# The feed-forward block's seven-product scheme: weight sums by adding transfers, and its first product behind the third plain chunk

## The chip, the core and the metric

One core of one Trainium2 chip runs the whole kernel. The metric is the device time in microseconds (us). Before the change it is 491.46 us, the median of 3 runs (491.43 to 491.74). Engines are called PE (TensorE: matrix multiplication), DVE (VectorE), ACT (ScalarE), POOL (GpSimd) and SP (SyncE, which issues most transfers here). Each engine works through its own list of instructions in order and waits on semaphores for the others.

## The reference

The kernel computes one decoder block for 256 tokens of width 1024: a gated linear recurrence and a block attention read the same normalised input, their outputs are gated, summed and projected, and a SwiGLU feed-forward block follows. Only that last block matters here (D = 1024, D_FF = 2816):

```
h2 = rmsnorm(x, ffn_norm_g[l])
x = x + (jax.nn.silu(h2 @ w_ffn_gate[l]) * (h2 @ w_ffn_up[l])) @ w_ffn_down[l]
```

## The kernel before

**Precision.** All products are float32 in effect. A float32 tensor is split into a high half (`whi`, made by an ACT copy to the reduced form float32r) and a low half (`wlo`, a DVE subtraction of the high half from the original); three products of halves replace one. `split` (L54 to L56) does this for activations and weights alike. A megabyte of weights (128 x 2048 elements) therefore costs one ACT copy and one DVE subtraction before PE can use it. The pools of halves (`whi`, `wlo`) and of raw weights (`wraw`) have three buffers each, so at most three blocks of weights are split ahead of PE or in use by it; a raw block is loaded by SP as soon as a raw buffer is free, that is, when an earlier block has been split.

**The feed-forward block.** Of the 2816 hidden columns the first 1792 (`NPL` = 14 tiles of 128) go the plain way, the last 1024 through a seven-product scheme.

- *Plain chunks.* `plain` (L798) makes gate and up columns in blocks of 512: two chunks of half the depth for the gate, two for the up weights. Each chunk is one call of `step(next, chunks_a)`, one load of 1 MB, one split, and 32 matmuls (16 of 512 columns at L102, 16 of 256 at L101 and L105). There are twelve such chunks, called c1 to c12 here, three blocks of four. After the second chunk of each pair the four PSUM banks are folded (L121, L122). A last short block (`rest`) follows.
- *The scheme.* `scheme` (L831) multiplies the 256 tokens by a 1024 x 1024 block of weights, cut into quarters W11, W12, W21, W22 of 512 x 512 and the tokens into halves. Instead of eight products of quarters it takes seven, P1 to P7, of sums of token blocks with sums of weight quarters. `quarter` (L629) loads a quarter (1 MB, SP), `halves` (L635) splits it, `product` (L641) issues 12 matmuls of 512 columns (L645). The token sums are made once by `token_sums2` (L783: four DVE operations of 128 x 512 and two splits) and serve both schemes. The weight sums are made by DVE, in place, between the products: four subtractions of 128 x 2048 (L841, L848, L853, L859) in each scheme.
- *Order.* The gate scheme is interleaved by hand with the twelve chunks: a string gives the order, "c" for a chunk and "P" for a product. Before, it is "ccPcPccPccPccPcPcPc". The up scheme is interleaved with the down projection's steps (`down`, one load of w_down, 24 matmuls at L903 to L905), one step before each product; PE goes D0, P1, D1, P2, D2, P3, D3, P4, D4 and so on.
- `tc.issue_after(x)` puts the instructions of its block behind x on x's engine. `step` uses it to keep PE to the written order. The lists of the other engines, the queues' included, are laid out by the framework from the written order and from when it expects operands to be free, so they may differ from the written order.

The tiles `T8` to `T11` hold the four quarters, first for the gate weights, then for the up weights; a quarter's load waits until the last reader of its tile is done.

Of the kernel before, what the change touches and what calls it, by code (L numbers as in the profile page):

```python
# [7 lines left out]
F32 = mybir.dt.float32  # L8
F32R = mybir.dt.float32r
U32 = mybir.dt.uint32  # L10
AF = mybir.ActivationFunctionType
OP = mybir.AluOpType
AX = mybir.AxisListType

P = 128
S = 256
# [11 lines left out]
def tile_hgrn2_moba_block(ctx: ExitStack, tc: tile.TileContext, xm, xw, table, runs,  # L28
                          w_in, w_hg, w_at, w_out, w_gate, w_up, w_down, out):
    nc = tc.nc  # L30
# [3 lines left out]
    small = ctx.enter_context(tc.tile_pool(name="small", bufs=1))  # L34
# [3 lines left out]
    def pw(name="pw"):  # L38
        return psum.tile([P, 512], F32, name=name, tag="pw", bufs=4)

    def ph(name="ph"):
        return psum.tile([P, 512], F32, name=name, tag="ph", bufs=2)

    def pa(name="pa"):
        return psum.tile([P, 512], F32, name=name, tag="pa", bufs=2)
# [8 lines left out]
    def split(src, hi, lo):  # L54
        high = nc.scalar.copy(hi, src)  # L55
        return high, nc.vector.tensor_sub(lo, src, hi.bitcast(F32))  # L56

    halved = []
# [80 lines left out]
    for kt in range(KT):  # L139
        n0 = 0 if kt == 0 else NV  # L140
        t = big.tile([P, NX + D - n0], F32, name=f"xw{kt}", tag=("T3", "T4", "T5", "T1", "T7", "T8", "T9", "T11")[kt])
# [29 lines left out]
    for kt in range(KT):  # L171
        i = kt % 2
# [11 lines left out]
        else:  # L184
# [3 lines left out]
                                       op0=OP.mult, op1=OP.subtract)  # L188
# [18 lines left out]
    for j in range(7):  # L207
        c = 1 << j
# [212 lines left out]
    def hgrn_out(A01):  # L421
        o = big.tile([P, 2, D], F32, name="o", tag="T2")
        so = small.tile([P, 2, H], F32, name="so")
        for tb in range(2):
            for g in range(2):
# [10 lines left out]
                nc.scalar.activation(o2.rearrange("p h t -> p (h t)"), bank, AF.Square)  # L436
                nc.vector.tensor_reduce(so[:, tb, 4 * g:4 * g + 4], o2, axis=AX.X, op=OP.add)
        ro = small.tile([P, 2, H], F32, name="ro")
# [81 lines left out]
    def softmax(nm, sc, w):  # L520
        mx = small.tile([P, H], F32, name="mx" + nm)
        nc.vector.tensor_reduce(mx, sc, axis=AX.X, op=OP.max)
        nc.vector.tensor_scalar_mul(mx, mx, -1.0)
# [74 lines left out]
    def branch_gate(br, half):  # L598
        ps = tok_block(w_in, 7168 + br * D + half * 512, XT)
        for tb in range(2):  # L600
            nc.scalar.activation(G[br][:, tb, half * 512:(half + 1) * 512], ps[tb], AF.Sigmoid,
                                 scale=rx[:, tb:tb + 1])
# [26 lines left out]
    def quarter(i, j, tag, w=w_in, c0=g0):  # L629
        t = big.tile([P, 4, 512], F32, name=f"W{i}{j}", tag=tag)  # L630
        nc.sync.dma_start(t, w[i * 512:(i + 1) * 512, c0 + j * 512:c0 + (j + 1) * 512]
                          .rearrange("(k p) c -> p k c", p=P))
        return t

    def halves(raw):  # L635
        hi = wp.tile([P, 4, 512], F32R, name="whi")
        lo = wp.tile([P, 4, 512], F32R, name="wlo")
        halved.append(split(raw, hi, lo))
        return hi, lo

    def product(bank, act, w, first):  # L641
        hi, lo = w
        for kt in range(4):
            for m, h in ((0, hi), (0, lo), (1, hi)):
                mm = nc.tensor.matmul(bank, act(kt, m), h[:, kt, :], start=(first and kt == 0 and m == 0 and h is hi),  # L645
                                      stop=(kt == 3 and m == 1), skip_group_check=True)
        tail[0] = mm
        return mm

    def tokens(i, j, act=XT):  # L650
        return lambda kt, m: act[j][:, kt, m, i * P:(i + 1) * P]

    def summed(c, of=None):
        return lambda kt, m: (of or sums)[m][c][:, kt, :]
# [5 lines left out]
    sums = token_sums()  # L660
    W11 = quarter(0, 0, "T9")
    W12 = quarter(0, 1, "T1")
    branch_gate(1, 1)
    turn_a, b1, turn_h, b3 = pa("turn"), pa("b1"), ph("turn"), ph("b3")
    product(b1, tokens(0, 0), halves(W11), True)
    oT, put_oT, at = hgrn_gate(o, ro, sg, (turn_a, turn_h, pw("turn"), pw("turn")))

    def then(f, *args):
        with tc.issue_after(at.ins):
            return f(*args)  # L670
# [24 lines left out]
    def gq(i, j):  # L695
        return G[0][:, i, j * 512:(j + 1) * 512]
# [4 lines left out]
    nc.scalar.copy(gq(1, 0), b1)  # L701
    nc.vector.tensor_sub(W11, W12, W11)
    step0, out0 = at_block(0)
    at = then(step0)
    at = then(product, b3, summed(0), halves(W11), True)
    W22 = quarter(1, 1, "T8")
    at = then(step0)
    with tc.issue_after(halved[-1][1].ins):
        nc.vector.tensor_sub(W11, W22, W11)
        low = nc.vector.tensor_sub(W12, W22, W12)  # L710
    put_oT(halved[-1][0], low)
    b2 = pa("b2")
    at = then(product, b2, summed(1), halves(W11), True)
    W21 = quarter(1, 0, "T2")
# [4 lines left out]
    with tc.issue_after(halved[-1][1].ins):  # L719
        out0()  # L720
        nc.vector.tensor_add(gq(0, 1), b2, gq(1, 0))
    at = then(product, b2, summed(2), halves(W12), False)
    nc.vector.tensor_add(gq(1, 1), b2, gq(1, 0))
# [32 lines left out]
    x2f = big.tile([P, 2, 4, S], F32, name="x2f", tag="T2")  # L756
    ss2 = small.tile([P, 2, 2], F32, name="ss2")
    for half in range(2):
        ps = tok_block(w_out, half * 512, M)
        for tb in range(2):  # L760
# [8 lines left out]
            x2_split = split(xg, x2T[half][:, :, 0, tb * P:(tb + 1) * P], x2T[half][:, :, 1, tb * P:(tb + 1) * P])  # L769
            jk2 = big.tile([P, 512], F32, name="jk2", tag="T15")  # L770
            nc.scalar.activation(jk2, xs, AF.Square, accum_out=ss2[:, tb, half:half + 1])
    r2 = small.tile([P, 2], F32, name="r2")
# [8 lines left out]
    SC = NPL * P  # L781

    def token_sums2():  # L783
        C = big.tile([P, 4, 4, P], F32, name="C2", tag="T3")
        hi = big.tile([P, 4, 4, P], F32R, name="C2h", tag="T4")
        lo = big.tile([P, 4, 4, P], F32R, name="C2l", tag="T5")
        nc.vector.tensor_add(C[:, 0], x2f[:, 0, :, P:S], x2f[:, 1, :, P:S])
        nc.vector.tensor_sub(C[:, 1], C[:, 0], x2f[:, 0, :, 0:P])
        nc.vector.tensor_sub(C[:, 2], x2f[:, 0, :, 0:P], x2f[:, 0, :, P:S])
        nc.vector.tensor_sub(C[:, 3], x2f[:, 1, :, 0:P], C[:, 1])  # L790
        for i in range(2):
            split(C[:, 2 * i:2 * i + 2], hi[:, 2 * i:2 * i + 2], lo[:, 2 * i:2 * i + 2])
        return [hi[:, c] for c in range(4)], [lo[:, c] for c in range(4)]

    def step(f, *args):
        with tc.issue_after(tail[0].ins):
            return f(*args)
# [32 lines left out]

    def scheme(w, banks, p1, at_out, q):  # L831

        X = x2T
        W11 = quarter(0, 0, "T10", w, SC)
        W21 = quarter(1, 0, "T9", w, SC)
        W12 = quarter(0, 1, "T11", w, SC)
        W22 = quarter(1, 1, "T8", w, SC)
        b1 = banks()
        product(b1, tokens(0, 0, X), halves(W11), True)
        nc.scalar.copy(p1, b1)  # L840
        nc.vector.tensor_sub(W11, W12, W11)  # L841
        yield
        product(b1, tokens(0, 1, X), halves(W21), False)
        at_out(0, 0, b1)
        yield
        b3 = banks()
        product(b3, summed(0, sums2), halves(W11), True)
        nc.vector.tensor_sub(W11, W22, W11)  # L848
        yield
        b2 = banks()  # L850
        product(b2, summed(1, sums2), halves(W11), True)
        nc.vector.tensor_add(q(0, 1), b2, p1)
        nc.vector.tensor_sub(W12, W22, W12)  # L853
        yield
        product(b2, summed(2, sums2), halves(W12), False)
        nc.vector.tensor_add(q(1, 1), b2, p1)
        nc.vector.tensor_add(q(1, 1), q(1, 1), b3)
        at_out(1, 1, q(1, 1))
        nc.vector.tensor_sub(W21, W21, W11)  # L859
        yield  # L860
        product(b3, summed(3, sums2), halves(W22), False)
        nc.vector.tensor_add(q(0, 1), q(0, 1), b3)
        at_out(0, 1, q(0, 1))
        yield
        product(b2, tokens(1, 1, X), halves(W21), False)
        nc.vector.tensor_add(q(1, 0), b2, p1)
        at_out(1, 0, q(1, 0))
        yield
# [53 lines left out]
    def gq2(i, j):  # L922
        return sG[:, i, j * 512:(j + 1) * 512]

    def silu(i, j, src):
        nc.scalar.activation(gq2(i, j), src, AF.Silu, scale=r2[:, i:i + 1])

    ring = iter([pa, ph, pa])
    blocks = iter([c for b in range(3) for c in [plain(4 * b, 4, b)]])
    chunks_a = (c for g in blocks for c in g)  # L930
    with tc.issue_after(x2_split[0].ins), tc.issue_after(x2_split[1].ins):
        sums2 = token_sums2()
    gate = scheme(w_gate, lambda: next(ring)("g"), gq2(1, 0), silu, gq2)
    for what in "ccPcPccPccPccPcPcPc":
        if what == "c":
            step(next, chunks_a)
        else:
            with tc.issue_after(x2_split[0].ins), tc.issue_after(x2_split[1].ins):
                step(next, gate)
    assert not list(chunks_a) and not list(gate)  # L940
    rest = plain(12, 2, 3)
    for _ in range(4):
# [5 lines left out]
    def uq(i, j):  # L948
        return U[:, i, j * 512:(j + 1) * 512]

    def hidden(i, j, src):
        nc.vector.tensor_mul(uq(i, j), src, gq2(i, j))

    def turn(i, j):
        bank = pw("turn")
# [85 lines left out]
```

## Time and profile before

| | before |
|---|---|
| median of 3 runs | 491.46 us |
| profiled execution: its own time | 492.7 us |
| profiled execution: span | 491.0 us |
| PE busy | 484.0 us (99%) |
| DVE busy | 397.8 us (81%) |
| ACT busy | 301.5 us (61%) |
| POOL busy | 24.8 us (5%) |
| moved by transfers | 91.16 MB, mean 186 GB/s |
| granted TensorE clock | 0.999 |

The profile is of one execution. A row of the timeline gives start and duration in us, the engine, the source line, the operation, out<-in by tile names, shapes, the count, and in brackets how long the engine had been idle before it and what it waited for. PE's matmuls overlap in the pipeline: a 512-column matmul is shown with 0.39 us, while the next one starts 0.23 us later. A row of the table of waits gives the total, the number of times and the longest wait. A transfer's issue row ends with the median time from issue to landing. The feed-forward block begins at about 306 us of the span.

### The profile page before, as it was taken

The numbers are of one execution on the slowest core, as the hardware profiler recorded it, in microseconds if no ns is written. First come the engines' busy times: TensorE is split into PE (matmuls) and PEld (weight loads), VectorE is DVE, ScalarE is ACT, GpSimd is POOL, SyncE is SP. The second block draws the span as 40 slices with busy tenths as digits, with TensorE's granted clock in tenths as the row PEclk, the third lists the DMA queues.
The fourth block names the chain that finished last, engine by engine and source line by source line (L and its number), as shares of the span: only waits on it lengthen the run. The fifth ranks groups of instructions, "written<-read, shape, count | busy, mean of one in ns | idle before, by whom it ended". The sixth has DMA issues, their size and how long they took to land.

```text
span 491.0 us, 6512 instructions
## 1 busy us (share of the span) xinstructions
PE 484.0 (99%) x2598; PEld 407.4 (83%) x2598; DVE 397.8 (81%) x426; ACT 301.5 (61%) x402; POOL 24.8 (5%) x59
## 2 busy tenths in 40 slices
PE   8999999999999999999999999989999999999997
PEld 6888888888888888988888878878888888888885
DVE  5768999697779979499987777999978779986843
ACT  5977746777748984875564445866565566454520
POOL 0930220000000000000000000000000000000000
PEclk9999999999999999999999999999999999999999
DMA  8977595724524448418367577433785564352402
GB/s 303 402 238 258 166 313 178 240 90 143 201 87 145 137 137 274 167 46 297 90 237 274 175 258 259 165 117 141 241 261 179 176 257 156 102 172 85 171 1 85
DMA packets 42142, 91.16 MB, mean 186 GB/s; under 512 B 1656, under 2 KB 3960, under 8 KB 42112
## 3 DMA queue, kind: packets, MB, share of 16 engines
q1 hardware_dynamic: 41376, 88.11, 52.7%
q0 software_dynamic: 736, 2.65, 1.7%
q8 instruction: 20, 0.33, 0.3%
q14 instruction: 10, 0.08, 0.0%
HBM read 89.67 MB, written 1.07 MB: 185 GB/s over the span
## 4 chain that ended last, share of the span: by engine, by line
PE 94%; DVE 4%; DMA 1%; ACT 0%; SPq 0%; issue 0%
PE pw L102 15%; PE pw L84 10%; PE pw L86 10%; PE pw L85 10%; PE pw L168 4%; PE acc L905 4%; PE acc L904 4%; PE acc L903 4%; PE pw L645 4%; PE b L645 4%; PE pw L105 4%; PE pw L101 4%; PE g L645 3%; PE pw L684 1%; PE pw L685 1%; PE pw L683 1%
## 5 line engine op out<-in xcount | busy, mean ns | idle before, releaser
L56 DVE TENSOR_TENSOR wlo<-wraw,whi 128x2048 fp32r<-128x2048 f32 (+1 forms) x69 | 149.0, 2164 | 39.2 <-ACT whi L55 39.0
L55 ACT CAST whi<-wraw 128x2048 fp32r<-128x2048 f32 (+1 forms) x69 | 124.7, 1813 | 61.7 <-PE pw L86 32.3
L102 PE MATMUL pw<-x2T,whi 128*128 128x512 f32 x224 | 71.8, 396 | 0.0
L56 DVE TENSOR_TENSOR wlo<-W,whi 128x2048 fp32r<-128x2048 f32 x21 | 47.9, 2287 | 11.1 <-ACT whi L55 11.0
L84 PE MATMUL pw<-whi,XT 128*128 128x512 f32 x144 | 56.9, 395 | 0.0
L55 ACT CAST whi<-W 128x2048 fp32r<-128x2048 f32 x21 | 40.2, 1913 | 26.5 <-PE acc L905 13.6
L86 PE MATMUL pw<-whi,XT 128*128 128x512 f32 x144 | 56.2, 390 | 0.0
L85 PE MATMUL pw<-wlo,XT 128*128 128x512 f32 x144 | 56.1, 390 | 0.0
L102 PE MATMUL pw<-XT,whi 128*128 128x512 f32 x128 | 40.6, 395 | 0.0
L102 PEld LDWEIGHTS pw<-x2T,whi 128*128 128x128 f32 x224 | 35.1, 189 | 0.5
L105 PE MATMUL pw<-x2T,wlo 128*128 128x256 f32 x112 | 31.3, 279 | 1.6 <-DVE wlo L56 1.6
L86 PEld LDWEIGHTS pw<-whi,XT 128*128 128x128 f32 x144 | 27.0, 188 | 5.7
L84 PEld LDWEIGHTS pw<-whi,XT 128*128 128x128 f32 x144 | 27.0, 188 | 5.6
L85 PEld LDWEIGHTS pw<-wlo,XT 128*128 128x128 f32 x144 | 27.1, 188 | 5.4
L101 PE MATMUL pw<-x2T,wlo 128*128 128x256 f32 x112 | 31.2, 279 | 0.0
L105 PEld LDWEIGHTS pw<-x2T,wlo 128*128 128x128 f32 x112 | 21.1, 188 | 6.5 <-DVE wlo L56 2.0
L101 PEld LDWEIGHTS pw<-x2T,wlo 128*128 128x128 f32 x112 | 21.0, 188 | 5.0
L903 PE MATMUL acc<-whi,hT 128*128 128x512 f32 x56 | 21.9, 391 | 0.0
L905 PE MATMUL acc<-whi,hT 128*128 128x512 f32 x56 | 21.8, 390 | 0.0
L904 PE MATMUL acc<-wlo,hT 128*128 128x512 f32 x56 | 21.8, 389 | 0.0
L102 PEld LDWEIGHTS pw<-XT,whi 128*128 128x128 f32 x128 | 19.8, 189 | 0.2
L168 PE MATMUL pw<-whi,XT 128*128 128x512 f32 x64 | 18.1, 400 | 0.7 <-ACT whi L186 0.7
(357 smaller groups left out, 1020.8 us busy)
## 6 DMA issues: line engine op xcount, KB each, us to landing
wraw<-w_in SPq DMA_DIRECT2D x26, 1024.0 KB, 5.1
wraw<-w_down SPq DMA_DIRECT2D x11, 1024.0 KB, 4.9
wraw<-w_gate SPq DMA_DIRECT2D x6, 1024.0 KB, 5.0
wraw<-w_up SPq DMA_DIRECT2D x6, 1024.0 KB, 5.1
wraw<-w_at SPq DMA_DIRECT2D x4, 1024.0 KB, 6.4
W<-w_in SPq DMA_DIRECT2D x4, 1024.0 KB, 5.3
wraw<-w_hg SPq DMA_DIRECT2D x4, 1024.0 KB, 5.7
W<-w_gate SPq DMA_DIRECT2D x4, 1024.0 KB, 6.0
```

The lines of the kernel that those rows point to most:

```text
L55: high = nc.scalar.copy(hi, src)
L56: return high, nc.vector.tensor_sub(lo, src, hi.bitcast(F32))
L84: nc.tensor.matmul(ps[tb], part(act, kt, 0)[:, ts], wh, start=(kt == 0), stop=False)
L85: nc.tensor.matmul(ps[tb], part(act, kt, 0)[:, ts], wl, start=False, stop=False)
L86: nc.tensor.matmul(ps[tb], part(act, kt, 1)[:, ts], wh, start=False, stop=(kt == KT - 1))
L101: nc.tensor.matmul(ps[ct][:, 0:S], lo[:, i, cs], part(act, kt, 0), start=False, stop=False)
L102: wide = nc.tensor.matmul(ps[ct], hi[:, i, cs], both, start=(kt == 0), stop=(kt == KT - 1))
L105: tail[0] = nc.tensor.matmul(ps[ct][:, 0:S], lo[:, i, cs], part(act, kt, 0), start=False, stop=False)
L645: mm = nc.tensor.matmul(bank, act(kt, m), h[:, kt, :], start=(first and kt == 0 and m == 0 and h is hi), stop=(kt == 3 and m == 1), skip_g ...
L903: nc.tensor.matmul(acc[tb][half], act[:, j, 0, ts], hi[:, i, cs], start=st, stop=False)
L904: nc.tensor.matmul(acc[tb][half], act[:, j, 0, ts], lo[:, i, cs], start=False, stop=False)
L905: tail[0] = nc.tensor.matmul(acc[tb][half], act[:, j, 1, ts], hi[:, i, cs], start=False, stop=en)
```

## The change

- The token sums change signs: the first is x2[1] − x2[0] of the second token half where it was a sum, and the second and fourth are formed by a scalar-tensor form (negate, then subtract). With that, every weight sum of the scheme is a plain sum. The second column half of the result comes out negated; `silu` takes a negated scale for it (`r2n`, one new operation of 128 x 2) and `hidden` multiplies by −1 in a scalar-tensor form.
- The eight DVE weight sums are gone. In their place a transfer on GpSimd's queue reads a quarter from HBM and adds it to a tile that holds another (`add`). Y is W11 loaded a second time; it becomes Y + W12 for P3, then + W22 for P4, then + W21 for P7. T3 is W22 loaded a second time, + W12, for P5. So each scheme has five plain loads on SP (W11, W21, Y, W22, T3) where it had four, and four adding transfers. Each is 1 MB.
- The order string becomes "cccsPcPccPcPccPcPcPc", where "s" makes the token sums. P1 moves from behind c2 to behind c3, P2 from behind c3 to behind c4, P3 from behind c5 to behind c6; P4 stays behind c7. The token sums and products are issued behind the split of c3, and c3 behind the split of the last token block.

```diff
@@ token_sums2
-        nc.vector.tensor_add(C[:, 0], x2f[:, 0, :, P:S], x2f[:, 1, :, P:S])
-        nc.vector.tensor_sub(C[:, 1], C[:, 0], x2f[:, 0, :, 0:P])
+        nc.vector.tensor_sub(C[:, 0], x2f[:, 1, :, P:S], x2f[:, 0, :, P:S])
+        nc.vector.scalar_tensor_tensor(C[:, 1], C[:, 0], -1.0, x2f[:, 0, :, 0:P], op0=OP.mult, op1=OP.subtract)
         nc.vector.tensor_sub(C[:, 2], x2f[:, 0, :, 0:P], x2f[:, 0, :, P:S])
-        nc.vector.tensor_sub(C[:, 3], x2f[:, 1, :, 0:P], C[:, 1])
+        nc.vector.scalar_tensor_tensor(C[:, 3], C[:, 1], -1.0, x2f[:, 1, :, 0:P], op0=OP.mult, op1=OP.subtract)
@@ scheme
+        def add(t, i, j):
+            nc.gpsimd.dma_start(t, w[i * 512:(i + 1) * 512, SC + j * 512:SC + (j + 1) * 512]
+                                .rearrange("(k p) c -> p k c", p=P), accum_op=OP.add)
+
         W11 = quarter(0, 0, "T10", w, SC)
         W21 = quarter(1, 0, "T9", w, SC)
-        W12 = quarter(0, 1, "T11", w, SC)
+        Y = quarter(0, 0, "T11", w, SC)
+        add(Y, 0, 1)
         W22 = quarter(1, 1, "T8", w, SC)
         b1 = banks()
         product(b1, tokens(0, 0, X), halves(W11), True)
         nc.scalar.copy(p1, b1)
-        nc.vector.tensor_sub(W11, W12, W11)
         yield
         product(b1, tokens(0, 1, X), halves(W21), False)
         at_out(0, 0, b1)
+        T3 = quarter(1, 1, "T10", w, SC)
+        add(T3, 0, 1)
         yield
         b3 = banks()
-        product(b3, summed(0, sums2), halves(W11), True)
-        nc.vector.tensor_sub(W11, W22, W11)
+        product(b3, summed(0, sums2), halves(Y), True)
+        add(Y, 1, 1)
         yield
         b2 = banks()
-        product(b2, summed(1, sums2), halves(W11), True)
+        product(b2, summed(1, sums2), halves(Y), True)
         nc.vector.tensor_add(q(0, 1), b2, p1)
-        nc.vector.tensor_sub(W12, W22, W12)
+        add(Y, 1, 0)
         yield
-        product(b2, summed(2, sums2), halves(W12), False)
+        product(b2, summed(2, sums2), halves(T3), False)
...
-        nc.vector.tensor_sub(W21, W21, W11)
...
-        product(b2, tokens(1, 1, X), halves(W21), False)
+        product(b2, tokens(1, 1, X), halves(Y), False)
@@ silu, hidden and the order
-        nc.scalar.activation(gq2(i, j), src, AF.Silu, scale=r2[:, i:i + 1])
+        nc.scalar.activation(gq2(i, j), src, AF.Silu, scale=(r2, r2n)[j][:, i:i + 1])
+    r2n = small.tile([P, 2], F32, name="r2n")
+    nc.vector.tensor_scalar_mul(r2n, r2, -1.0)
-    with tc.issue_after(x2_split[0].ins), tc.issue_after(x2_split[1].ins):
-        sums2 = token_sums2()
-    for what in "ccPcPccPccPccPcPcPc":
+    third, chunk_no = None, 0
+    for what in "cccsPcPccPcPccPcPcPc":
         if what == "c":
-            step(next, chunks_a)
-        else:
             with tc.issue_after(x2_split[0].ins), tc.issue_after(x2_split[1].ins):
+                step(next, chunks_a) if chunk_no == 2 else None
+            if chunk_no != 2:
+                step(next, chunks_a)
+            third = third or (halved[-1] if chunk_no == 2 else None)
+            chunk_no += 1
+            continue
+        with tc.issue_after(third[0].ins), tc.issue_after(third[1].ins):
+            if what == "P":
                 step(next, gate)
+            else:
+                sums2 = token_sums2()
-        nc.vector.tensor_mul(uq(i, j), src, gq2(i, j))
+        nc.vector.scalar_tensor_tensor(uq(i, j), src, (1.0, -1.0)[j], gq2(i, j), op0=OP.mult, op1=OP.mult)
```

## The prediction

> **What bounds the kernel now.** I read the page first, for busy shares and the chain that ended last.
>
> ```profile
> span 491.0 us, 6512 instructions
> ...
> PE 484.0 (99%) x2598; PEld 407.4 (83%) x2598; DVE 397.8 (81%) x426; ACT 301.5 (61%) x402; POOL 24.8 (5%) x59
> ...
> PE 94%; DVE 4%; DMA 1%; ACT 0%; SPq 0%; issue 0%
> ```
>
> TensorE (PE) is busy 484.0 of 491.0 us and the change leaves its multiplications as they are, so only its idle time can be won, 7.0 us in all. The windows view (stretch, length, then each engine's busy time, PE first) places it.
>
> ```profile
> 0.00:20.00 20.00, 18.20 (x76) 14.95 (x77) 12.71 (x32) 13.28 (x26) 8.58 (x22) 1.00 0.91 345
> 320.00:330.00 10.00, 8.40 (x45) 6.91 (x44) 10.00 (x9) 6.77 (x7) 0.00 (x0) 1.00 0.35 109
> 480.00:491.00 11.00, 7.36 (x39) 6.14 (x37) 3.94 (x6) 0.00 (x0) 0.00 (x0) 0.97 0.26 95
> ```
>
> PE idles 1.8 us at the start, 3.6 at the end and 1.6 in one hole between 320 and 330 us, with DVE busy all 10.0; these are the 7.0. Only the hole lies in the feed-forward stage, which alone the change touches. The table of waits and PE's timeline show it.
>
> ```profile
> PE pw L105 <- DVE wlo L56: 1.6, 1, 1.6
> ```
> ```profile
> 318.36 0.39 PE L645 MATMUL g<-whi,x2T 128*128 128x512 f32 x1
> ...
> 321.08 1.08 PE L102 MATMUL pw<-x2T,whi 128*128 128x512 f32 x4
> 323.76 0.39 PE L105 MATMUL pw<-x2T,wlo 128*128 128x256 f32 x1 [1.60 <-DVE wlo L56]
> ...
> 328.56 0.39 PE L645 MATMUL g<-whi,x2T 128*128 128x512 f32 x1
> ...
> 331.29 0.39 PE L102 MATMUL pw<-x2T,whi 128*128 128x512 f32 x1
> ...
> 342.44 0.39 PE L645 MATMUL g<-whi,C2h 128*128 128x512 f32 x1
> ```
>
> From 318.36 PE runs P1, from 321.08 the third plain chunk c3, from 328.56 P2, then c4 and c5 from 331.29 to 342.44. Two undisturbed chunks took 11.15 us, so one takes 5.57 and a product (318.36 to 321.08) 2.72. Chunk c3 took 328.56 − 321.08 = 7.48: **1.9 us too long**, because the low half of its weights came late. VectorE's (DVE) timeline says why.
>
> ```profile
> 309.49 0.68 DVE L787 TENSOR_TENSOR C<-x2f 128x512 f32<-128x512 f32 x1
> ...
> 311.30 2.28 DVE L56 TENSOR_TENSOR wlo<-W,whi 128x2048 fp32r<-128x2048 f32 x1
> ...
> 315.82 2.28 DVE L841 TENSOR_TENSOR W<-W,W 128x2048 f32<-128x2048 f32 x1
> ...
> 318.36 1.21 DVE L56 TENSOR_TENSOR C2l<-C,C2h 128x1024 fp32r<-128x1024 f32 x1
> ...
> 321.42 2.28 DVE L56 TENSOR_TENSOR wlo<-wraw,whi 128x2048 fp32r<-128x2048 f32 x1
> ```
> ```profile
> 308.75 1.91 ACT L55 CAST whi<-W 128x2048 fp32r<-128x2048 f32 x1
> ...
> 313.02 1.90 ACT L55 CAST whi<-wraw 128x2048 fp32r<-128x2048 f32 x1
> ```
>
> ScalarE had c3's high half at 314.9, after P1's (308.75), but DVE reached the low half (321.42) only after the token sums (309.49 to 318.36), P1's split and the first weight sum. DVE, not PE, was the bound for this stretch alone.
>
> **Part 1: c3 ahead of P1, token sums behind c3.** The split of c3 now takes the place, and the third weight buffer, that P1's split had: high half at 308.75, low half at 311.30 or sooner, so it is there by 313.6, and PE reaches c3 when c2 ends, at 318.36: 4.8 us of room where there was a hole. What is late next? P1's split: it needs c1's buffer, free when c2 begins, at the latest 318.36 − 5.57 = 312.8, and P1 now starts at 318.36 + 5.57 = 323.93; eleven us for 1.9 + 2.28. The token sums (four additions like the 0.68 and two splits like the 1.21, 5.1 us) are first used by P3 at 346. Adjacent c2 and c3 both need four PSUM banks, but c4 and c5 are such a pair and show no hole. Gain: **−1.9 us**. Between nothing (DVE's folds of c2 fill the place) and −1.9 I take −1.9, since 9.7 us of DVE work (5.1, P1's 2.28, the weight sum's 2.28) leave the stretch ahead of c3's low half and the room is 4.8.
>
> **Part 2: eight weight sums leave DVE.**
>
> ```profile
> L859 DVE TENSOR_TENSOR W<-W,W 128x2048 f32<-128x2048 f32 x2 | 4.6, 2286 | 0.0
> ...
> L841 DVE TENSOR_TENSOR W<-W,W 128x2048 f32<-128x2048 f32 x2 | 4.6, 2282 | 0.0
> ```
>
> These are the last and the first of four such groups: 8 × 2.28 = 18.3 us of DVE. Worth nothing beyond part 1, since PE has no other hole before the end of the span. The two scalar-tensor forms in the token sums, the negated r2 and the sign in `hidden` replace operations of equal size one for one, or add one on 128 x 2; I set them at nothing, covered by the 18.3 us given up.
>
> **Part 3: the adds.** Each scheme issues five plain loads on SP (four before) and four adds on GpSimd, 1 MB each. Nothing in the trace adds in a transfer. Nearest rows:
>
> ```profile
> wraw<-w_down SPq DMA_DIRECT2D x11, 1024.0 KB, 4.9
> ...
> x<-xm POOLq DMA_DIRECT2D x1, 1024.0 KB, 5.2
> ...
> line_d<-line POOLq DMA_DIRECT2D x1, 24.0 KB, 2.1
> ```
>
> A plain megabyte on GpSimd's queue lands after 5.2 us, 24 KB after 2.1, so the megabyte itself is 3.1. An add must read the tile as well as the source: two passes make 2.1 + 6.2 = 8.3 us, and three passes (two reads and a separate write) 11.4. The lower bound is 5.2. [...]
>
> Most adds have long cover. In the second scheme (up) Y's first load takes the buffer that a load had late in the list of before:
>
> ```profile
> 383.23 0.37 SPq L631 DMA_DIRECT2D W<-w_up  x1
> ```
>
> From there 5.2 and an add of up to 12.8 end near 401, and P3's split is at 420. Y's last add has P5 and P6 ahead of P7, T3's has P3 and P4 ahead of P5. The tight one is **Y += W22, between P3's split and P4's split**. It can't start before P3's halves are made (they read Y), and P4's halves can't start before it lands. In the up scheme:
>
> ```profile
> 420.00 1.92 ACT L55 CAST whi<-W 128x2048 fp32r<-128x2048 f32 x1 [3.04 <-PE acc L905]
> ...
> 428.21 1.92 ACT L55 CAST whi<-W 128x2048 fp32r<-128x2048 f32 x1 [3.57 <-PE acc L905]
> 430.93 1.92 ACT L55 CAST whi<-wraw 128x2048 fp32r<-128x2048 f32 x1 [0.80 <-PE pw L645]
> ```
> ```profile
> 421.95 2.29 DVE L56 TENSOR_TENSOR wlo<-W,whi 128x2048 fp32r<-128x2048 f32 x1 [1.17 <-ACT whi L55]
> ...
> 426.96 2.28 DVE L56 TENSOR_TENSOR wlo<-wraw,whi 128x2048 fp32r<-128x2048 f32 x1
> ```
> ```profile
> 436.12 0.39 PE L645 MATMUL pw<-whi,C2h 128*128 128x512 f32 x1
> 436.35 0.39 PE L645 MATMUL pw<-wlo,C2h 128*128 128x512 f32 x1
> ```
>
> P3's split ends at 421.95 + 2.29 = 424.24 and waits for PE's buffer (420.00), not for DVE, so it can't come earlier. P4's second matmul, at 436.35, needs a low half, 1.92 + 2.29 after the add landed: by 432.14. The window is **7.9 us**. (All of this moves by the 1.9 together.) The add takes 8.3 alone, and w_down's load for a later step is issued when DVE ends the low half at 426.96, which without the sum ahead of it moves up by 2.28 to about 427, into the middle of the add. Sharing the engines with that load's 4.9 − 2.1 = 2.8 us costs the add about half of it, 1.4. So 9.7 us, 1.8 more than the window: **+1.8 us** on PE at P4. Ends: 5.2 gives 0; 11.4 + 1.4 = 12.8 gives 4.9. Behind P4's waiting split on ScalarE stands the next step's (430.93); PE asks for it only when P4 has ended, 2.72 us after P4's start, however late that is, so its own 1.92 and 2.28 stay covered.
>
> In the first scheme (gate) there is a chunk pair ahead of P3, so its split is earlier:
>
> ```profile
> 334.01 2.29 DVE L56 TENSOR_TENSOR wlo<-W,whi 128x2048 fp32r<-128x2048 f32 x1 [0.90 <-ACT whi L55]
> ```
>
> That ended 336.30 − 331.29 = 5.0 us after P2. New times: P1 ends at 326.65, c4 332.22, P2 334.94, so the split ends at 339.95; c5, c6, P3, c7 follow, and P4 starts at 354.37. Needed by 354.60 − 4.2 = 350.4: window 10.4, against 9.7. No stall; with 12.8, 2.4 us.
>
> **The sum.** −1.9 + 1.8 + 0 = −0.1 us on the profiled 491.0. That execution took 492.7 with 1.7 us around its span; the runs' median is 491.46. Forecast: 491.46 − 0.1 = **491.4 us**. About 0.2%, 1.0 us, is what a measurement here can tell from no change: the forecast means a stall between 0.9 and 2.9 us.
>
> **The rivals.**
> *Adds inside the window.* If two reads overlap, or w_down's load doesn't share, the add lands within 7.9 to 8.8 us and the hole is won: 491.46 − 1.9 = 489.6. For it: 8.3 alone is only 0.4 over the window. Against: the load at 427.
> *Adds slower than two passes* (the slower side). At three passes both windows break: −1.9 + 4.9 + 2.4 = +5.4, 496.9 us. It decides from a landing of about 10.8 us. For it: an add is a form without any row here. Against: the plain transfer's 3.1 us per megabyte.
> *T3's add stands ahead on GpSimd's queue.* It needs T3's load, whose buffer is free after P1's split. SP works through its list in order:
>
> ```profile
> SPq L67 <- DVE wlo L56: 309.3, 56, 18.8
> ```
>
> If T3's load stands behind a w_down load that waits (up to 18.8 us, here), T3's add is still moving data when Y's is issued, and delays it by up to its own 6.2 us; at half, 3.1, the stall is 4.9: +3.0, 494.5. Against it: T3's buffer is free one split before that load's.
> *GpSimd's issue is held while DVE works.* Held for one 2.28 us operation, the add lands at 12.0: stalls of 4.1 (up) and 1.6 (gate), +3.8, 495.3.
>
> ```profile
> 243.34 0.70 POOL L740 DMA_DIRECT2D x<-xm  x1 [174.58 <-DVE wlo L56]
> ```
> ```profile
> 242.96 2.29 DVE L56 TENSOR_TENSOR wlo<-wraw,whi 128x2048 fp32r<-128x2048 f32 x1
> ```
>
> Against it: x's load was issued in 0.70 us, in the middle of a DVE operation of 2.29. [...]
> *The reorder has no effect:* c3's low half still falls behind folds; without the gain 493.3.
>
> **Chances.** Forecast 0.38; adds inside the window 0.30; slower adds 0.17; T3 ahead 0.07; issue held 0.03; no reorder 0.03; 0.02 for no change by another way. Faster is the second, 0.30; same 0.40; slower the other four, 0.30. The forecast's own range is 490.5 to 492.4. The range, 489.5 to 495.5, takes in the full gain, T3 and the held issue, and slower adds up to a landing of 12 us or so; it leaves out about 0.12.
>
> **What would show it.** Right: c3's wait on wlo gone and 5.6 us for it; about 18 us less on DVE; 10.5 MB more read from HBM (two loads and eight adds); adds landing in 8 to 10 us; PE waiting on a split of W right at the up scheme's P4, 1 to 3 us, and nowhere else. Wrong: adds landing under 7.9 or over 11 us, a wait at the gate's P4, at P5 (T3) or at P7, or c3 still late.

## The result, and the profile after

The changed kernel takes 496.71 us (median of 6 runs; 493.35 to 497.08 in five of them), beside 491.61 us for the kernel before (6 runs, 491.43 to 492.15). The ratio is 1.0084 with a 95% interval of 1.0062 to 1.0105: slower by 4 us, where 491.4 us (489.5 to 495.5) was forecast. The sixth run, at a granted clock of 0.62, took 731.59 us; it and two such runs of the last experiment are left out of the comparisons.

The profiled execution took 496.99 us, with a span of 495.3 (before: 492.7 and 491.0). Its page, engines first, then GpSimd's queue:

```profile
span 495.3 us, 6541 instructions
PE 486.5 (98%) x2598; PEld 408.9 (83%) x2598; DVE 381.2 (77%) x419; ACT 300.9 (61%) x402; POOL 35.9 (7%) x67
DMA packets 47422, 101.65 MB, mean 205 GB/s; under 512 B 1816, under 2 KB 4120, under 8 KB 47392
W<-w_gate POOLq DMA_DIRECT2D x4, 1024.0 KB, 10.8
W<-w_up POOLq DMA_DIRECT2D x4, 1024.0 KB, 10.7
```

The change did what it says: DVE has 16.6 us less (397.8 to 381.2), and 10.5 MB more move (91.16 to 101.65). The eight adds land 10.7 to 10.8 us after their issue, in the median. Where PE lost time is seen in the windows view (stretch, length, then busy time of PE, its weight loads, DVE, ACT and POOL, the granted clock, the busy share of the transfer engines, GB/s):

```profile
320.00:330.00 10.00, 10.00 (x56) 8.60 (x55) 8.67 (x6) 7.62 (x9) 1.27 (x1) 1.00 0.61 206
350.00:360.00 10.00, 7.91 (x40) 6.16 (x39) 5.18 (x3) 7.11 (x6) 1.29 (x1) 1.00 0.30 82
430.00:440.00 10.00, 8.06 (x35) 6.15 (x34) 3.31 (x2) 5.25 (x3) 0.73 (x1) 1.00 0.56 159
440.00:450.00 10.00, 10.00 (x40) 8.07 (x40) 6.28 (x4) 3.23 (x3) 0.56 (x1) 0.83 0.92 213
440.57:443.99 3.42, 3.42 (x10) 2.65 (x9) 3.41 (x3) 1.14 (x1) 0.00 (x0) 0.50 0.82 119
```

The hole at c3 (320 to 330 us, PE 8.40 before) is gone. Two new holes of 2 us stand at 350 to 360 and 430 to 440, and behind the second one PE runs at half clock for 3.4 us. PE's table of waits names both holes, one in each scheme:

```profile
PE pw L645 <- DVE wlo L56: 1.8, 1, 1.8
PE g L645 <- DVE wlo L56: 1.8, 1, 1.8
```

Both are P4, and both have the same chain behind them: the add's issue on POOL, ACT's high half as soon as it has landed, DVE's low half, then PE's second matmul. First POOL's timeline (the first three rows are the gate scheme's adds: W12 to Y, W12 to T3, then Y += W22; the last two are the up scheme's T3 and Y += W22):

```profile
289.25 1.36 POOL L837 DMA_DIRECT2D W<-w_gate  x1 [45.65 <-DMA W<-w_gate]
328.73 1.30 POOL L837 DMA_DIRECT2D W<-w_gate  x1 [38.13 <-ACT whi L55]
340.13 1.28 POOL L837 DMA_DIRECT2D W<-w_gate  x1 [10.10 <-DVE wlo L56]
...
415.40 1.28 POOL L837 DMA_DIRECT2D W<-w_up  x1 [24.80 <-DMA W<-w_up]
424.90 1.28 POOL L837 DMA_DIRECT2D W<-w_up  x1 [8.21 <-DVE wlo L56]
```

ACT's, at the two P4:

```profile
352.33 1.91 ACT L55 CAST whi<-W 128x2048 fp32r<-128x2048 f32 x1 [6.19 <-DMA W<-w_gate]
...
434.75 1.91 ACT L55 CAST whi<-W 128x2048 fp32r<-128x2048 f32 x1 [9.79 <-DMA W<-w_up]
```

PE's, at the same places:

```profile
353.63 0.40 PE L102 MATMUL pw<-x2T,whi 128*128 128x512 f32 x1
354.29 0.50 PE L645 MATMUL g<-whi,C2h 128*128 128x512 f32 x1 [0.26 <-ACT whi L55]
356.62 0.50 PE L645 MATMUL g<-wlo,C2h 128*128 128x512 f32 x1 [1.82 <-DVE wlo L56]
...
436.21 0.39 PE L912 MATMUL acc<-whi,hT 128*128 128x512 f32 x1
436.71 0.49 PE L645 MATMUL pw<-whi,C2h 128*128 128x512 f32 x1
439.03 0.50 PE L645 MATMUL pw<-wlo,C2h 128*128 128x512 f32 x1 [1.83 <-DVE wlo L56]
```

Matmuls start 0.23 us apart, so without the wait the second matmul of P4 would start 0.46 us after the last one shown ahead of P4: at 354.09 and 436.67. It starts at 356.62 and 439.03. The stalls are **2.5 us (gate) and 2.35 us (up)**. The adds landed 352.33 − 340.13 = 12.2 us after the issue in the gate scheme and 434.75 − 424.90 = 9.85 in the up scheme (9.75 by the chain's own row, which ends at the landing).

The span's +4.3 us, piece by piece: −1.9 (hole at c3), +2.5 and +2.35 (the two P4), +1.7 (3.42 us at a clock of 0.50), and −0.5 because the feed-forward block began a little earlier in this execution (its first matmul at 305.35, before at 305.86). Together +4.15.

### The profile page after: what moved, and what is told of

It is laid out like the page before. It is cut to its first block, busy times and chain, and to the rows that moved or that the text cites. A ratio compares the mean times of both kernels' runs of the same rounds, so it can differ in the third digit from the quotient of the medians.

```text
span 495.3 us, 6541 instructions
## 1 busy us (share of the span) xinstructions
PE 486.5 (98%) x2598; PEld 408.9 (83%) x2598; DVE 381.2 (77%) x419; ACT 300.9 (61%) x402; POOL 35.9 (7%) x67
## 2 busy tenths in 40 slices
DMA packets 47422, 101.65 MB, mean 205 GB/s; under 512 B 1816, under 2 KB 4120, under 8 KB 47392
```

## The experiments

All are timed beside the kernel before on the same chip (medians of 491.65 to 491.9 us there); the ratios are to it. The diffs are against the changed kernel. The theory was that the loss is the serial chain P3's split, add, P4's split; the rivals were GpSimd's issue held up by DVE, the transfer engines being busy in general, the reorder itself, and the adds' extra traffic.

**The reorder alone**, with the old scheme and DVE's weight sums.

```diff
-        Y = quarter(0, 0, "T11", w, SC)
-        add(Y, 0, 1)
+        W12 = quarter(0, 1, "T11", w, SC)
...
+        nc.vector.tensor_sub(W11, W12, W11)
...
```

> Only the new order (first product and token sums behind the third plain chunk); the weight sums stay on VectorE, no adding transfer. Theory A (the changed kernel loses its time in two waits of P4 for the add of W22, 2.5 us in the gate scheme and 2.35 in the up scheme, and in 1.7 us of half clock behind the second; the reorder itself gains 1.9): 491.6 - 1.9 = 489.7 us, c3 takes 5.6 us, no hole between 320 and 330 us, clock 1.0. Rival B (10.5 MB more traffic slows the whole block): also 489.7 here, since no traffic is added. Rival C (the reorder gains nothing of its own, the hole closed only because VectorE lost its sums): 491.6 us, with c3 or the next products late.

Measured: 490.37 us, ratio 0.9968 (0.9955 to 0.998), 1.5 us less than before. The window of the hole:

```profile
320.00:330.00 10.00, 9.70 (x53) 8.05 (x52) 10.00 (x8) 8.13 (x9) 0.00 (x0) 1.00 0.17 43
```

PE went from 8.40 to 9.70; with DVE still busy all 10.0 us, 0.3 us of the wait is left. The reorder is not what made the kernel slower.

**P4's sum on DVE in both schemes**, the six other adds kept.

```diff
-        add(Y, 1, 1)
+        nc.vector.tensor_add(Y, Y, W22)
```

> The changed kernel, but the one sum Y + W22 between P3 and P4 is a VectorE addition in both schemes; the other six adds stay transfers. Theory A: both waits and the half clock vanish, 489.7 us (489.2 to 490.3), no PE wait on a split of W at P4. Rival B (traffic): six of eight adds remain, so three quarters of the loss stay, 494 to 495 us.

Measured: 489.92 us, ratio 0.9956 (0.9944 to 0.9969); no wait at either P4. So the whole loss, 4 us and 2 more, hangs on two of the eight adds. This version beats both kernels.

**A plain transfer in the add's place.**

```diff
-        add(Y, 1, 1)
+        nc.gpsimd.dma_start(Y, w[512:1024, SC + 512:SC + 1024].rearrange("(k p) c -> p k c", p=P))
```

> The changed kernel, but the transfer between P3 and P4 copies W22 over Y and does not add (this leaves out a part of the sum): same queue, same bytes from HBM, same waits. It prices the adding itself. Theory A: it lands in 5 to 7 us in the up scheme, inside the window of 7.9, and inside 10.4 in the gate scheme, so no PE wait: 489.7 us. If the wait were for the queue's issue and order and not for the second read, the landing would stay at 9 to 12 us and the time at 493 to 497.

This version leaves out a part of the sum (Y is overwritten and not added to). Measured: 489.5 us, ratio 0.9952 (0.994 to 0.9965), no wait of PE at P4. Landing of the two transfers at this place, then of the changed kernel's eight adds:

```profile
DMA to landing us min/median/max: 5.4/6.7/8.0
```
```profile
DMA to landing us min/median/max: 8.8/10.7/13.4
```

The plain megabyte lands after 8.0 us in the gate scheme and 5.4 in the up scheme, where the adds took 12.1 and 9.7 by the same view. The same chain with it fits the windows of 10.4 and 7.9 us; it is the add's own length that breaks them.

**P4's sum on DVE, with the add's traffic kept** (added to a tile that nothing reads afterwards).

```diff
-        add(Y, 1, 1)
+        nc.vector.tensor_add(Y, Y, W22)
+        add(W21, 1, 1)
```

> As the run with Y + W22 on VectorE, but the same megabyte is still added by transfer at the same place, into the tile of W21, which nobody reads any more: all eight adds move their bytes, only the wait for one of them is gone. Theory A: 489.7 us, as without it. Rival B (traffic): 494 to 497 us, like the changed kernel.

Measured: 489.69 us, ratio 0.9952 (0.9938 to 0.9965), no wait. The framework placed the extra add earlier than meant (next to T3's, in both schemes), so the traffic is the same in sum but not in its minute. With that limit: eight adds that PE does not wait for cost no more here than six (489.69 us against 489.92).

**The add in two halves**, each half split as it lands.

```diff
...
-        add(Y, 1, 1)
+        add(Y, 1, 1, 2)
...
-        product(b2, summed(1, sums2), halves(Y), True)
+        product(b2, summed(1, sums2), halves(Y, 2), True)
```

> The changed kernel, but the add of W22 between P3 and P4 comes as two adds of half a megabyte, and P4's split as two splits of half the size: the first half is split while the second still lands. Theory A (only the wait counts): the second half may land 2.1 us later than before since its split is half as long, and 1.4 us later again since it is first used at P4's seventh matmul: windows of 11.3 us (up) and 13.9 us (gate) against landings of 9.8 and 12.2. No wait, 489.6 to 490.3 us beside 491.9 for the kernel before. Rival B (traffic): 494 to 497 us, since all eight adds move their bytes.

Measured: 492.24 us, ratio 1.001 (1.0002 to 1.0019). A miss. The gate's wait went, but the up scheme's wait only moved. ACT's timeline there, and PE's waits:

```profile
427.60 1.05 ACT L55 CAST whi<-W 128x1024 fp32r<-128x1024 f32 x1 [5.93 <-DMA W<-w_up]
433.00 1.05 ACT L55 CAST whi<-W 128x1024 fp32r<-128x1024 f32 x1 [4.35 <-DMA W<-w_up]
433.96 1.90 ACT L55 CAST whi<-wraw 128x2048 fp32r<-128x2048 f32 x1
```
```profile
PE acc L915 <- DVE wlo L56: 1.2, 1, 1.2
...
PE pw L647 <- DVE wlo L56: 0.5, 1, 0.5
```

The first half lands 6.0 us after the issue (421.61), the second 11.4. PE works on the first half meanwhile and waits only 0.5 us for the second; but the split of the next step's weights (433.96) is queued behind the second half on ACT, and PE, no longer held up at P4, asks for it 1.2 us too early.

**The add in the gate scheme only, and in the up scheme only** (P4's other sum on DVE).

```diff
-        add(Y, 1, 1)
+        if w is w_up:
+            nc.vector.tensor_add(Y, Y, W22)
+        else:
+            add(Y, 1, 1)
```

> The changed kernel with Y + W22 on VectorE in the up scheme alone; the gate scheme keeps its add. Theory A: one wait of about 2.5 us at the gate's P4, 491.9 - 2.1 + 2.5 = 492.3 us with a full clock. If a wait of this length also brings the half clock for 3.4 us, 494.0 us. Rival D (the half clock has nothing to do with the waits): the clock falls here as often as in the changed kernel.

Measured: 492.4 us (490.9 to 494.56), ratio 1.0011 (0.9997 to 1.0026).

> The changed kernel with Y + W22 on VectorE in the gate scheme alone; the up scheme keeps its add. Theory A: one wait of about 2.35 us at the up scheme's P4, 491.9 - 2.1 + 2.35 = 492.2 us with a full clock, and 493.9 us where the granted clock falls to 0.50 for 3.4 us behind that wait, as in the profile of the changed kernel. Rival D: the clock never falls, or falls elsewhere.

Measured: 493.55 us, ratio 1.003 (1.0019 to 1.0041). Each has its own P4's wait and not the other's. Against 489.92 without either, the medians stand 2.5 and 3.6 us higher: the two losses of the changed kernel are separate, and either alone spends the 2 us won.

**The adds with the old order.**

```diff
-    for what in "cccsPcPccPcPccPcPcPc":
+    for what in "ccPcPccPccPccPcPcPc":
...
```

> All eight adds, but the old order (P1 behind the second chunk, token sums at the front). P3 then has two chunks between it and P4 and not one, so the gate scheme's window is 10.4 + 5.6 = 16 us and its wait should be gone; the hole at c3 should close to a few tenths, since the first weight sum no longer stands on VectorE ahead of c3's low half. Theory A: only the up scheme's wait is left: 491.9 - 1.6 + 2.35 = 492.7 us, 494.4 with the half clock. Rival B (traffic): 495 us or more, with all adds and no reorder.

Measured: 493.98 us, ratio 1.004 (1.0026 to 1.0054). The gate's wait is gone. In the old order two chunks stand between P3 and P4, not one; but T3's add is also issued earlier there, 15.5 us before Y += W22 (318.36 and 333.82; 11.4 us in the changed kernel), and Y += W22 has landed when ACT takes it at 342.74, within 8.9 us and not 12.2. By the numbers either would have been enough, and this run does not separate them. The up scheme's wait stays, again with half clock behind it (0.83 over ten us). And, against what the prediction takes for granted, the hole at c3 is gone too, without the reorder. Both in the windows view:

```profile
320.00:330.00 10.00, 10.00 (x55) 8.61 (x54) 7.82 (x6) 8.03 (x8) 0.00 (x0) 1.00 1.08 282
```
```profile
430.00:440.00 10.00, 8.01 (x28) 5.98 (x27) 6.36 (x3) 5.50 (x3) 1.28 (x1) 0.83 0.40 104
```

**T3's add behind Y += W22 on GpSimd's queue**, in both schemes.

```diff
...
-        add(T3, 0, 1)
...
-        add(Y, 1, 1)
+        with tc.issue_after(add(Y, 1, 1).ins):
+            add(T3, 0, 1)
```

> The changed kernel with one edit: T3's add is issued behind Y += W22 on GpSimd's queue, so that its megabyte is no longer moving when the gate scheme's Y += W22 is issued. Theory (the gate's landing of 12.2 us came from T3's add and the loads still on the transfer engines, where the up scheme's add, issued with less beside it, took 9.75): the gate's add lands within about 10 us and PE's wait at the gate's P4 (1.8 us on the low half, 2.5 in all) shrinks below 0.5 us; the wait at the up scheme's P4 stays near 1.8. About 2.5 us less than the changed kernel, so 492.5 to 494.5 us, depending on how often half clock follows. Risk: T3 is late for P5, a new wait there. Rival (the gate's add is slow by itself, whatever is queued ahead of it): landing stays near 12, the wait stays, 496 us.

Measured: 491.49 us, ratio 0.9998 (0.9989 to 1.0006). The gate's wait is gone and the up scheme's is still there, as the theory has it. POOL's timeline (each row the two adds together), ACT's, and PE's waits:

```profile
339.35 2.60 POOL L837 DMA_DIRECT2D W<-w_gate  x2 [49.65 <-DVE wlo L56]
...
421.35 2.59 POOL L837 DMA_DIRECT2D W<-w_up  x2 [34.44 <-DVE wlo L56]
```
```profile
348.24 1.91 ACT L55 CAST whi<-W 128x2048 fp32r<-128x2048 f32 x1 [2.89 <-DMA W<-w_gate]
...
430.75 1.91 ACT L55 CAST whi<-W 128x2048 fp32r<-128x2048 f32 x1 [9.34 <-DMA W<-w_up]
```
```profile
PE pw L645 <- DVE wlo L56: 1.8, 1, 1.8
```

The gate's add now lands by 348.24 − 339.35 = 8.9 us, where it took 12.2 with T3's add ahead of it; the up scheme's by 9.4. SP's loads ahead of it are the same (five issued from 322.19 to 335.65, in the changed kernel from 323.00 to 336.44), and T3's add still moves, right behind it: T3's add ahead of it was what made the difference. T3's own adds land later (15.9 us at most) and PE does not wait for them at P5. The time is 1.0 us below the range expected (492.5 to 494.5), because half clock never followed the wait that is left: all 11 executions have a clock of 1.0.

**A wait of PE made without a transfer**: P4's sums on DVE, and four copies on ACT ahead of the up scheme's P4.

```diff
-        add(Y, 1, 1)
+        nc.vector.tensor_add(Y, Y, W22)
+        if w is w_up:
+            for _ in range(4):
+                nc.scalar.copy(Y, Y)
```

> P4's sum on DVE in both schemes, and in the up scheme four in-place copies of Y on ScalarE (1.9 us each, 7.6 in all) ahead of P4's split, so that PE waits about 2 us there without any adding transfer in the dependency. Theory (the half clock of 3.41 us follows any such wait of PE): 489.9 + 2.0 = 491.9 us in executions at full clock and about 493.6 in those where half clock follows; the mean granted clock of its executions falls to 0.995 or so in part of them. Rival (the half clock belongs to the adding transfers or to their load on the chip): the clock stays at 0.998 to 1.0 in all executions and the time at 491.9.

Measured: 494.21 us, ratio 1.0052 (1.004 to 1.0064), and a clock of 0.993 to 0.997 in all five executions. PE's timeline and a window of it:

```profile
433.93 0.50 PE L645 MATMUL pw<-whi,C2h 128*128 128x512 f32 x1 [0.57 <-ACT whi L55]
436.25 0.80 PE L645 MATMUL pw<-wlo,C2h 128*128 128x512 f32 x1 [1.82 <-DVE wlo L56]
436.84 0.63 PE L645 MATMUL pw<-whi,C2l 128*128 128x512 f32 x1
437.27 0.63 PE L645 MATMUL pw<-whi,C2h 128*128 128x512 f32 x1
...
439.72 0.39 PE L645 MATMUL pw<-whi,C2h 128*128 128x512 f32 x1
```
```profile
436.00:440.00 4.00, 3.75 (x10) 3.02 (x11) 4.00 (x3) 1.47 (x1) 1.28 (x1) 0.57 0.38 44
```

After the wait the matmuls start 0.43 us apart instead of 0.23, for some 3 us. By the window, 4.00 × 0.43 = 1.7 us are lost. The half clock follows the wait, with no add in the dependency. Six adds still move here, but the same six without the four copies (the 489.92 us above) left the clock at 0.999 or 1.0 in all five executions: the rival, that the transfers bring it, falls. The stall itself was 2.8 us (433.43 to 436.25), 0.8 more than meant.

**The changed kernel again.**

> The changed kernel once more, beside the two others on the same chip: 495 to 497 us. Both theories expect the same; it gives a second profile to see whether the waits at the two P4 (2.5 and 2.35 us in the first) and the half clock behind one of them recur at the same places. Theory (half clock follows a wait, by chance): the waits recur at both, the half clock may sit at the other or be missing.

Measured: 495.37 us, ratio 1.0085 (1.0062 to 1.0107). Both waits of 1.8 us recur at the two P4; the profiled execution (clock 0.999) had no half clock behind either, the others' clocks lie between 0.993 and 1.0.

**The old order with P4's sum on DVE** (the two edits above together).

> The changed kernel with the order of before (ccPcPccPccPccPcPcPc, no chunk ahead of P1) and P4's sum on DVE in both schemes: six adding transfers, no reorder. The profile of the run with eight adds and the old order showed PE busy all of 320 to 330 us, so either edit may close the hole at c3 by itself. Theory (the hole goes as soon as the first weight sum, 2.28 us, leaves DVE there; the reorder adds nothing to that): no wait at c3, 489.7 to 490.3 us, the same as with the reorder and P4's sum on DVE (489.92). Rival (the reorder is needed): a wait of 0.5 us or more at c3 and 490.5 to 491.5 us.

Measured: 489.67 us, ratio 0.9953 (0.9938 to 0.9967). No wait at c3; DVE's timeline has c3's low half (the `wraw` row) 6.4 us earlier than the 321.42 of before:

```profile
312.67 0.67 DVE L790 SCALAR_TENSOR_TENSOR C<-C,x2f 128x512 f32<-128x512 f32 x1
...
315.00 2.28 DVE L56 TENSOR_TENSOR wlo<-wraw,whi 128x2048 fp32r<-128x2048 f32 x1
```

In DVE's list the low half now has the place that the first weight sum had (315.82 before), ahead of a token split and of folds which came before it then. The reorder adds nothing once the first weight sum has left DVE: this is the time of the same adds with the reorder, 489.92, within their intervals. It beats both kernels too.

## Why the prediction was wrong, by its own steps

- **Part 1, −1.9 us:** right in size: −1.5 by the reorder alone, −2.0 with six adds. The attribution was half of the truth. "Worth nothing beyond part 1" holds, but so does the reverse: with the sums gone, part 1 is worth nothing beyond part 2.
- **Part 2:** right, within some tenths. DVE gave up 16.6 us where 18.3 were counted; P7 had no wait, and neither had P5, even with T3's add issued later.
- **The up scheme's P4, +1.8:** right. A landing of 9.7 us was forecast and 9.75 measured, with w_down's load issued at 427.43, where 427 was expected. The window was 7.4 to 7.5 where 7.9 was worked out, so the stall was 2.35. That the landing splits into 8.3 and 1.4 of sharing is not shown by any run.
- **The add's price:** 8.3 us, two passes, was the author's estimate, and the landing of 9.7 us worked out with it held in the up scheme alone. At the same place add and plain megabyte landed after 9.7 and 5.4 us (up) and 12.1 and 8.0 (gate); less the 2.1 us of the 24 KB transfer that is 7.6 against 3.3 and 10.0 against 5.9, 2.3 and 1.7 times as long. How many passes an add makes, and how the reads and writes of a transfer overlap, no run shows.
- **The gate scheme's P4: this is the step that failed**, "window 10.4, against 9.7. No stall". The 9.7 was worked out in the up scheme, from what is on the transfer engines there (one w_down load), and carried over. In the gate scheme SP's loads come closer together (six issues from 323.0 to 344.5 us; in the up scheme one every 8 to 14 us). T3's add, issued among them at 328.73, took 13.4 us, to 342.1, and so was still moving when Y's was issued at 340.13, with the transfer engines full (a share of 1.05): Y's landed after 12.2 us. In the up scheme T3's add took 8.8 us and had landed at 424.2, before Y's was issued at 424.90; the share in the four us from there was 0.73. The window itself was also narrower than worked out, 12.2 − 2.5 = 9.7 us and not 10.4. Windows of the changed kernel, then of the one with T3's add behind:

```profile
336.00:340.00 4.00, 4.00 (x25) 3.47 (x25) 3.83 (x4) 1.51 (x1) 0.00 (x0) 1.00 1.09 262
340.00:344.00 4.00, 4.00 (x25) 3.51 (x24) 1.82 (x1) 2.55 (x3) 1.28 (x1) 1.00 1.05 381
...
425.00:429.00 4.00, 4.00 (x20) 3.30 (x19) 2.40 (x2) 0.00 (x0) 1.18 (x1) 1.00 0.73 151
```
```profile
339.35:344.00 4.65, 4.65 (x29) 4.07 (x28) 2.61 (x3) 2.92 (x4) 2.60 (x2) 1.00 0.68 145
```

With T3's add behind, the share there is 0.68, the landing 8.9 and the stall gone. Whether Y's data waits in the queue for the rest of T3's, or both only share the engines, no run here shows. The rival "T3's add stands ahead" was this mechanism; it was given 0.07 and priced at the up scheme's P4, where it does not act. The whole forecast, −1.9 + 1.8 + 0, is what the kernel with T3's add behind shows: 491.49 us, no change. Of the 4.4 us between the forecast's −0.1 and the profile's +4.3, 2.5 are this step, 1.7 the half clock below, 0.5 the size of the up scheme's stall, and −0.5 the earlier start of the block; 0.2 are not placed. The rival "Adds slower than two passes" came near the time (496.9 us), but by luck: it has stalls of 4.9 (up) and 2.4 (gate) and no half clock, and in the up scheme the add was not slower than forecast.
- **The reorder narrowed the very window that broke.** The prediction gave 10.4 us for the new order and never asked for the old one, where c6 and c7 both stand between P3 and P4: 5.57 us more. With the old order the gate's wait is gone, though there T3's add is issued further ahead as well.
- **A term that was missing: half clock.** A stall was priced at its own length. In 27 of the 41 executions of the five kernels whose profiles show a stall of 2.35 to 2.8 us at P4 (the changed kernel, timed twice, and four of the experiments), the granted clock was 0.997 or lower; in none of the others (the kernel before, and the seven kernels with no stall there or one under 2 us) was it below 0.998. Each of the two stretches measured costs 1.7 us. Shown: with a wait of PE made without an add in the dependency the clock was 0.993 to 0.997 in all five executions, without that wait 0.999 or 1.0 in all five. Open: why some executions of the same kernel keep the full clock.
- **The next step's split "stays covered"** held in the changed kernel, and failed as soon as P4 was no longer held up whole: in the run with halves it cost 1.2 us.

## What to carry to other kernels

An in-place sum between two consumers is a chain: the reader's last split, the add, the next split; compare the landing *under the load of that place* with the window, each place by itself, and look at what the same queue issued just ahead. Give adding transfers the sums that nobody waits for, and leave the tight one on the engine that does it sooner: here DVE, in 2.28 us, where the adds landed after 9.7 and 12.1. Price a wait of PE above its length: here stalls of 2.35 to 2.8 us came with a lower clock in 27 of 41 executions, at 1.7 us for each stretch measured, and one of 1.9 us in none of 11.

## What the runs showed of the hardware

- A wait of PE of 1.8 us behind a single matmul, with 0.2 to 0.6 us of idle ahead of that matmul, was followed by 3.42 us at a granted clock of 0.50 in the changed kernel's profile (up scheme), by some 3 us with matmuls 0.43 us apart in that of the wait made without a transfer, and by none in that of the changed kernel's second timing, which has both waits; the 1.8 us that were left with T3's add behind, with nothing ahead of the matmul, left the clock at 1.0 in all 11 executions.
- An add of 1 MB held POOL for 1.28 to 1.36 us at its issue in the changed kernel (`x`'s plain megabyte 0.70), and its eight landed after 8.8 us at best, 10.7 in the median. The gate's T3 add, among SP's loads, took 13.4, the longest of the eight; in the second timing the longest took 14.5. With T3's add behind Y += W22 the longest took 15.9. No issue was held up by DVE's work: the one at 328.73 took 1.30 us beside a DVE operation of 2.29.
